# Two-layer decoder trunk on one core: the last dots moved ahead of the one-hot stage, value reads issued there, and a reordered RMSNorm

## Chip, cores and metric

One NeuronCore of a Trainium2 chip runs the whole program in one launch. The metric is device time in microseconds (us), the median of several runs. The program's engines are TensorE (PE; its weight loads are listed as PEld), VectorE (DVE), ScalarE (ACT), GpSimd (POOL) and SyncE (SP), which only issues DMAs here.

## What is computed

The reference runs two layers over 256 tokens of width 1024, then a final RMSNorm. A layer is: modulated RMSNorm, a token mixer (two kinds of attention, fed by one projection), a gated residual add, a second modulated RMSNorm, PEER expert retrieval and a second residual add. The part that the change touches most is PEER:

```
def rms_norm(x, g):
    y = x * lax.rsqrt(jnp.mean(x * x, axis=-1, keepdims=True) + RMS_EPS)
    return y * g
...
q = (ht @ wq).reshape(PEER_CHUNK, PEER_HEADS, 2, half)       # 8 heads
...                                                          # product keys: 16 of 16384 experts a head
act = jax.nn.gelu(jnp.einsum('td,thkd->thk', ht, u[e]))
return jnp.einsum('thk,thkd->td', gate * act, v[e])
```

Every token needs 8 x 16 = 128 rows of u and as many of v, out of tables of 16384 rows of 1024 floats each.

## The kernel before, in words

The kernel keeps the activations transposed in `xT` (eight tiles of 128 features by 256 tokens). One function writes each engine's instructions in the order of the source; nothing reorders them, and each engine and each DMA queue works through its own list in that order.

**PEER is done in two ways at once.** For the first 160 tokens (`ND`) TensorE multiplies with the whole tables: 128 tiles of u (512 KB each, 128 experts by 1024 features), a one-hot stage that turns the chosen experts and gates into a dense gate matrix, then 128 tiles of v. For the last 96 tokens (`NG`) GpSimd reads only the chosen rows by indirect DMA, 128 rows (512 KB) a read, 96 reads of u and 96 of v a layer. VectorE takes the dot product of each u read with the tokens (`dot`, L1236), ScalarE and VectorE turn the dots into weights (`weigh` L1240, `gated` L1243), and VectorE adds each v read, weighted, into one of two accumulators (`axpy`, L1250 and L1252). A v read can be issued when a dot or an axpy has given a buffer back; up to ten are in flight.

**In the order of the program**, `peer` has: 16 query units (L1351 to L1372); 128 u tiles (L1444), each followed by a Gelu on ScalarE (L1432) and by gather work that a build-time account of VectorE's time lets in (`fill`); the one-hot stage (L1456 to L1475), 40 rounds of four tokens, each with three one-hots on VectorE and one on GpSimd (L1409), a matmul (L1416, `spread_gates`) and a multiplication into the dense matrix on VectorE (L1475); 128 v tiles (L1506). The six queued tiles of v and ten more in spare memory are loaded in the one-hot stage, so sixteen lie ready when the v tiles begin.

Beside the v tiles the gather work that is left runs at a pace, `V_PACE`: a credit of 0.7 steps a tile up to tile 106 and 1.2 after it. Before each such step VectorE copies one column of the newest v tile asked for (`seen`, L1510), so that a step, and with it the read that it lets go, waits until that tile has landed. At tile 122 (`NI - GE`) all steps that are left are issued without that wait. After tile 124 (`NI - GP`) `gathered_part` (L1485) has TensorE fold the two accumulators onto the tokens (L1491): first the one whose buffer is named side, then the one named rows, each when its last axpy is done. Two tiles follow, then the sums of squares of the 96 tokens (L297), the last tile, the residual adds (L1482), the squares of the 160 tokens (L288) and their sums (L297).

**RMSNorm** is `rms_rstd` (L306): the sums of squares lie in a PSUM bank; ScalarE takes the reciprocal root of sum/1024 + epsilon (L312), VectorE forms sum/1024 + epsilon again (L313) and does one Newton step with it (L314 to L316). `busy` (L299) gives TensorE `W1` or `W2` idle matmuls beside that. `norm_mod` then forms the scale `gs` (L325) and the normalised tiles; after the mixer `norm_whole` (L352) makes them.

**Weights** pass through `feed` (L371): a loaded piece is cut into a high part on ScalarE (L395) and a low part, a subtraction on VectorE or GpSimd (L397). Ahead of the norm after the mixer, `want(pos[U_WQ])` (L1581) makes sure that three query units are cut, the third one's subtraction included.

## Time and profile before

| what | value |
|---|---|
| median of 3 runs | 1949.45 us (1948.42 to 1951.34) |
| the profiled execution's own time | 1956.64 us |
| its span | 1954.8 us |
| busy share of the span | PE 95%, PEld 91%, DVE 66%, POOL 29%, ACT 26% |
| data moved | 605.26 MB, mean 310 GB/s |
| mean granted TensorE clock | 0.971 of full |

All rows come from the profiled execution. Start times count from the start of its span. A timeline row is: start, duration, engine, line, operation, what it writes and reads, how many were merged, and in brackets the idle time just before it with what ended it. A TensorE operation in 32-bit floats has two records a matmul, so one v or u tile (eight matmuls) is 16 records.

### The profile page before, as it was taken

What the parts mean: (1) busy time and instruction counts of PE and PEld (TensorE: products, weight loads), DVE (VectorE), ACT (ScalarE), POOL (GpSimd) and SP (SyncE); (2) the same over time, 40 slices, a digit from 0 to 9 for tenths busy, and PEclk for the clock granted to TensorE, in tenths of its full rate; (3) what the DMA queues carried; (4) which work ended last, traced back from release to release, by engine and by line L of the source; (5) the groups of instructions that cost most, each with busy time, mean ns of one, the idle gap of its engine ahead of it and who ended that gap; (6) DMA issues with size and microseconds to landing.
All of it is one profiled execution on the core that took longest, in us unless ns stands there. A gap on an engine that the chain in (4) does not pass through costs nothing. (4 is left out here: it accounts for less than half of the span.)

```text
span 1954.8 us, 34450 instructions
## 1 busy us (share of the span) xinstructions
PE 1857.3 (95%) x13284; PEld 1779.2 (91%) x13284; DVE 1288.4 (66%) x3084; ACT 500.4 (26%) x1079; POOL 573.4 (29%) x524
## 2 busy tenths in 40 slices
PE   5899999999999999999879999999999999999996
PEld 4778898999999899999868799899999998999995
DVE  8788765789854854444765987578995458344456
ACT  3444545211211710000025554522111154000001
POOL 4000005245443533322400000243454344322341
PEclk7899999999999999999989999999999999999997
DMA  7767656899999379999926574589999974999993
GB/s 274 282 229 261 218 162 240 325 386 365 409 408 409 140 270 375 409 409 408 407 96 240 204 267 163 200 294 366 366 409 408 409 295 145 349 408 408 407 410 155
DMA packets 166484, 605.26 MB, mean 310 GB/s; under 512 B 18480, under 2 KB 19120, under 8 KB 166192
## 3 DMA queue, kind: packets, MB, share of 16 engines
q1 hardware_dynamic: 111024, 401.71, 54.8%
q0 software_dynamic: 55296, 201.35, 26.3%
q8 instruction: 105, 1.72, 0.4%
q14 instruction: 59, 0.48, 0.1%
HBM read 601.94 MB, written 1.05 MB: 308 GB/s over the span
## 5 line engine op out<-in xcount | busy, mean ns | idle before, releaser
L1506 PE MATMUL bank<-wide,piece 128*128 128x160 f32 x3904 | 535.8, 300 | 2.6 <-DVE wide L1475 2.6
L1506 PEld LDWEIGHTS bank<-wide,piece 128*128 128x128 f32 x3904 | 534.4, 191 | 3.0 <-DVE wide L1475 3.0
L1444 PE MATMUL bank<-whole,piece 128*128 128x160 f32 x2624 | 360.7, 299 | 0.7 <-issue 0.4
L1444 PEld LDWEIGHTS bank<-whole,piece 128*128 128x128 f32 x2624 | 357.5, 190 | 1.6 <-issue 1.6
L1215 POOL DMA_INDIRECT side<-in_u_dram,routes x140 | 164.1, 1172 | 263.5 <-DVE side L1236 161.6
L397 POOL TENSOR_TENSOR piece<-piece 128x1024 fp32r<-128x1024 f32 x28 | 68.2, 2442 | 530.3 <-ACT piece L395 526.9
L1510 DVE COPY seen<-piece 128x1 f32<-128x1 f32 x176 | 27.0, 153 | 294.1 <-DMA piece<-in_v_dram 285.8
L1215 POOL DMA_INDIRECT side<-in_v_dram,routes x134 | 135.3, 1010 | 281.2 <-DVE side L1252 170.1
L1444 PE MATMUL bank<-whole,wide 128*128 128x160 f32 x1472 | 205.5, 299 | 3.1 <-issue 3.1
L1444 PEld LDWEIGHTS bank<-whole,wide 128*128 128x128 f32 x1472 | 201.3, 190 | 3.6 <-issue 3.4
L1432 ACT ACTIVATE wide<-bank 128x160 f32<-128x160 f32 x256 | 77.7, 305 | 469.3 <-PE bank L1444 406.0
L420 PE MATMUL bank<-hHL,piece 128*128 128x256 f32 (+1 forms) x592 | 176.7, 299 | 17.5 <-ACT hHL L344 14.2
L421 PE MATMUL bank<-hHL,piece 128*128 128x256 f32 (+1 forms) x592 | 174.9, 295 | 5.5 <-POOL hHL L347 4.3
L422 PE MATMUL bank<-hHL,piece 128*128 128x256 f32 (+1 forms) x592 | 173.5, 293 | 4.5 <-DVE piece L397 3.4
L395 ACT ACTIVATE piece<-piece 128x1024 fp32r<-128x1024 f32 x140 | 146.3, 1062 | 98.6 <-issue 37.3
L397 DVE TENSOR_TENSOR piece<-piece 128x1024 fp32r<-128x1024 f32 (+1 forms) x112 | 138.3, 1240 | 49.5 <-ACT piece L395 43.3
L1236 DVE SCALAR_TENSOR_TENSOR side<-side 128x1024 f32<-128x1024 f32 x94 | 114.9, 1222 | 45.0 <-DMA side<-in_u_dram,routes 35.1
L420 PEld LDWEIGHTS bank<-hHL,piece 128*128 128x128 f32 (+1 forms) x592 | 117.5, 199 | 20.4 <-ACT hHL L344 15.1
L421 PEld LDWEIGHTS bank<-hHL,piece 128*128 128x128 f32 (+1 forms) x592 | 117.2, 198 | 9.4 <-POOL hHL L347 6.4
L422 PEld LDWEIGHTS bank<-hHL,piece 128*128 128x128 f32 (+1 forms) x592 | 117.5, 199 | 6.5 <-DVE piece L397 4.9
L1252 DVE SCALAR_TENSOR_TENSOR side<-side,routes 128x1024 f32<-128x1024 f32 x86 | 110.5, 1285 | 0.4 <-DMA side<-in_v_dram,routes 0.3
L261 DVE SCALAR_TENSOR_TENSOR wide<-wide 128x1024 f32<-128x1024 f32 x80 | 97.7, 1222 | 16.9 <-DMA wide<-in_w_ada_dram 16.9
(244 smaller groups left out, 2777.8 us busy)
## 6 DMA issues: line engine op xcount, KB each, us to landing
piece<-in_v_dram SPq DMA_DIRECT2D x244, 512.0 KB
piece<-in_uT_dram SPq DMA_DIRECT2D x164, 512.0 KB
piece<-in_W_dram SPq DMA_DIRECT2D x147, 512.0 KB
wide<-in_uT_dram SPq DMA_DIRECT2D x92, 512.0 KB
wide<-in_w_ada_dram SPq DMA_DIRECT2D x80, 512.0 KB
side<-in_w_ada_dram SPq DMA_DIRECT2D x16, 512.0 KB
wide<-in_v_dram SPq DMA_DIRECT2D x8, 512.0 KB
side<-in_u_dram,routes POOLq DMA_INDIRECT x140
```

Source lines behind the costliest of these rows:

```text
L261: nc.vector.scalar_tensor_tensor(buf(n), buf(n), 1.0, self.S["silu"], op0=OP.mult, op1=OP.mult, accum_out=self.mod[l][:, u:u + 1])
L395: nc.scalar.activation(Hs[i], raws[i], AF.Copy)
L397: self.subs.append(lambda: eng.tensor_sub(Ls[i], raws[i], Hs[i].bitcast(F32)))
L420: mm(out, l[0], r[0], start=start, stop=False, skip_group_check=True)
L421: mm(out, l[0], r[1], start=False, stop=False, skip_group_check=True)
L422: mm(out, l[1], r[0], start=False, stop=stop, skip_group_check=True)
L1215: nc.gpsimd.indirect_dma_start(out=r, out_offset=None, in_=self.a[table], in_offset=bass.IndirectOffsetOnAxis(ap=self.gidx[:, lot:lot + 1] ...
L1236: nc.vector.scalar_tensor_tensor(junk, box[n], 1.0, htok[a], op0=OP.mult, op1=OP.mult, accum_out=dots[:, lot:lot + 1])
L1252: nc.vector.scalar_tensor_tensor(acc[a], box[n], dots[:, lot:lot + 1], acc[a], op0=OP.mult, op1=OP.add)
L1432: nc.scalar.activation(dst(i - 1), ps.pop(i - 1)[:, :ND], AF.Gelu_apprx_tanh)
L1444: nc.tensor.matmul(p[:, :ND], w[:, k], self.whole[:, k, :ND], start=(k == 0), stop=(k == KC - 1))
L1506: nc.tensor.matmul(acc[k], r[:, k * 128:(k + 1) * 128], dst(i), start=i == 0 and k % 2 == 0, stop=i == NI - 1, skip_group_check=True)
```

## The change

It has three parts.

- **Gather.** At the last u tile the remaining dots, `weigh` and `gated` are issued at once, then `pump` issues reads of v into every free buffer. `V_PACE` becomes 1.25 a tile for 8 tiles and 0.74 after that, and the `seen` copy is left out for the first 8 tiles.
- **Norms.** Epsilon times 1024 is added to the sums by a matmul of one row (`epsd`), the first into the bank, so the root needs no bias and the Newton step reads the bank itself: L313 goes. The scale `gs` is formed ahead of the root (`norm_scale`). At the end of PEER the squares go to memory of the gather stage instead of a ring of three tiles. `W1` is 13 for 16 and `W2` 8 for 10. A copy at the start that nothing used (`identr`) goes.
- **Third query unit.** Its subtraction is put behind the norm's work, and its 24 matmuls are ordered so that the eight with the low part come last.

The diff, cut:

```
-W1 = 16
-W2 = 10
+W1 = 13
+W2 = 8
-V_PACE = (0.7, 106, 1.2)
+V_PACE = (1.25, 8, 0.74)
+        self.epsd = cp.tile([1, 128], F32, name="epsd")
+        nc.gpsimd.memset(self.epsd, EPS * D)
-    def sum_sq(self, k, lo=0, hi=SEQ):
-
-        sq = self.wk.tile([128, SEQ], F32, name="sq", tag="t2", bufs=3)[:, :hi - lo]
+    def sum_sq(self, k, lo=0, hi=SEQ, sq=None):
+
+        if sq is None:
+            sq = self.wk.tile([128, SEQ], F32, name="sq", tag="t2", bufs=3)[:, :hi - lo]
...
-            self.ss, start = self.bank(), True
-        else:
-            start = False
-        self.nc.tensor.matmul(self.ss[:, lo:hi], self.ones, sq, start=start, stop=k == KC - 1, skip_group_check=True)
+            self.ss = self.bank()
+            self.nc.tensor.matmul(self.ss[:, :SEQ], self.epsd, self.ones[0:1, 0:1].to_broadcast([1, SEQ]), start=True,
+                                  stop=False, skip_group_check=True)
+        self.nc.tensor.matmul(self.ss[:, lo:hi], self.ones, sq, start=False, stop=k == KC - 1, skip_group_check=True)
...
-        nc.scalar.activation(r, p, AF.Abs_reciprocal_sqrt, bias=self.epst, scale=1.0 / D)
-        nc.vector.tensor_scalar(v, p, 1.0 / D, EPS, op0=OP.mult, op1=OP.add)
+        nc.scalar.activation(r, p, AF.Abs_reciprocal_sqrt, scale=1.0 / D)
         nc.vector.tensor_mul(q, r, r)
-        nc.vector.scalar_tensor_tensor(q, q, -0.5, v, op0=OP.mult, op1=OP.mult)
+        nc.vector.scalar_tensor_tensor(q, q, -0.5 / D, p, op0=OP.mult, op1=OP.mult)
...
+    def norm_scale(self, l, which):
+
+        g = self.vec[:, V_L + l * V_LN + 48 + 8 * which:][:, :8]
+        self.gs = self.wk.tile([128, 8], F32, name="gs", tag="gs")
+        self.nc.vector.scalar_tensor_tensor(self.gs, self.mod[l][:, 24 * which + 8:24 * which + 16], 1.0, g, op0=OP.add,
+                                            op1=OP.mult)
...
+        if low_last:
+            for n, (a, b) in enumerate([(0, 0), (0, 1), (1, 0)]):
+                for k in range(KC):
+                    self.nc.tensor.matmul(out, w[a][:, k], self.h[k][:, b], start=n == 0 and k == 0,
+                                          stop=n == 2 and k == KC - 1, skip_group_check=True)
+            return
...
-                self.proj_T(p[:, :SEQ], w)
+                self.proj_T(p[:, :SEQ], w, low_last=j == 2)
...
+                if i == NI - 1:
+                    while self.weighed < 2 and gather():
+                        pass
+                    head(gathers)
+                    self.pump()
...
-            if credit[0] > 0 and head(gathers) is not None and i < NI - 9:
+            if credit[0] > 0 and head(gathers) is not None and V_PACE[1] <= i < NI - 9:
                 nc.vector.tensor_copy(seen, ahead[max(ahead)][:, 0:1])
...
-            sums.append(self.sum_sq(k, 0, ND))
+            sums.append(self.sum_sq(k, 0, ND, G[:, UNIT + k * ND:UNIT + (k + 1) * ND]))
...
+        self.put_off = True
         want(pos[U_WQ])
+        self.put_off = False
         self.norm_mod(l, 1)
+        self.flush()
```

What the diff does not tell is how many steps move. GpSimd's list around the one-hot stage (both layers alike; L1215 is the indirect read and L1409 the one-hot, in the changed file L1227 and L1423) is before:

```order
L1215 DMA side<-in_u_dram,routes 128x1024 x5
L1215 DMA rows<-in_v_dram,routes 128x1024
L1409 TENSOR_SCALAR piece<-cst,routes 128x128 x5
L1215 DMA rows<-in_v_dram,routes 128x1024
L1409 TENSOR_SCALAR piece<-cst,routes 128x128 x35
L1215 DMA side<-in_v_dram,routes 128x1024 x6
```

and now:

```order
L1227 DMA side<-in_u_dram,routes 128x1024 x5
L1227 DMA rows<-in_v_dram,routes 128x1024 x2
L1227 DMA side<-in_v_dram,routes 128x1024 x6
L1227 DMA rows<-in_v_dram,routes 128x1024
L1227 DMA side<-in_v_dram,routes 128x1024
L1423 TENSOR_SCALAR piece<-cst,routes 128x128 x40
```

Ten reads of v stand ahead of all 40 one-hots where one stood before, with a second after five one-hots. On VectorE at the same place (dots L1248, `gated` L1256, one-hots L1423, multiplication L1494 in the changed file), the changed list is:

```order
L1248 SCALAR_TENSOR_TENSOR side,routes<-rows 128x1024 x2
L1248 SCALAR_TENSOR_TENSOR side,routes<-side,rows 128x1024 x5
L1256 TENSOR_TENSOR routes<-routes 128x96
L1423 TENSOR_SCALAR piece<-cst,routes 128x128 x9
L1494 TENSOR_TENSOR wide<-wide,bank 128x128x4
```

The five dots and `gated` (L1256) stood behind the 40 rounds before, among the first v tiles. VectorE's list at the end of the v tiles of the first layer (copy `seen` L1510, axpy L1252, cut L397) is before:

```order
L1510 COPY seen<-piece 128x1
L1252 SCALAR_TENSOR_TENSOR rows<-side,routes,rows 128x1024 x5
L397 TENSOR_TENSOR piece<-wide,piece 128x1024 x2
L1252 SCALAR_TENSOR_TENSOR rows<-side,routes,rows 128x1024
L1252 SCALAR_TENSOR_TENSOR rows<-rows,routes 128x1024
L1252 SCALAR_TENSOR_TENSOR rows<-side,routes,rows 128x1024
L1252 SCALAR_TENSOR_TENSOR rows<-rows,routes 128x1024 x2
L1252 SCALAR_TENSOR_TENSOR rows<-side,routes,rows 128x1024 x4
```

and now (copy L1529, axpy L1266, cut L402):

```order
L1529 COPY seen<-piece 128x1
L1266 SCALAR_TENSOR_TENSOR rows<-rows,routes 128x1024
L1266 SCALAR_TENSOR_TENSOR rows<-side,routes,rows 128x1024 x3
L402 TENSOR_TENSOR piece<-wide,piece 128x1024 x2
L1266 SCALAR_TENSOR_TENSOR rows<-side,routes,rows 128x1024
```

Behind the last copy stood 14 axpys and now stand 5; nine more have a copy of their own ahead of it. The second layer is the same without the two cuts.

## Rows read from the trace of the kernel before

**Rows 1.** The page, its 40 equal slices of the span (48.9 us each): GB/s that the DMA engines moved.

```profile
GB/s 274 282 229 261 218 162 240 325 386 365 409 408 409 140 270 375 409 409 408 407 96 240 204 267 163 200 294 366 366 409 408 409 295 145 349 408 408 407 410 155
```

**Rows 2.** Waits of PE over the whole span: who waited for whom, us in total, times, longest.

```profile
PE bank L1491 <- DVE rows L1252: 27.5, 2, 16.3
PE bank L420 <- ACT hHL L344: 14.2, 2, 12.9
```

**Rows 3.** Timeline, end of the v tiles of the second layer (DVE and PE).

```profile
1910.14 0.15 DVE L1510 COPY seen<-piece 128x1 f32<-128x1 f32 x1 [1.17 <-DMA piece<-in_v_dram]
1910.24 7.89 DVE L1252 SCALAR_TENSOR_TENSOR rows<-side,routes,rows 128x1024 f32<-128x1024 f32 x6
...
1915.76 1.89 PE L1491 MATMUL bank<-cst,side 128*128 128x64 f32 x16
...
1923.45 5.25 DVE L1252 SCALAR_TENSOR_TENSOR rows<-side,routes,rows 128x1024 f32<-128x1024 f32 x4
...
1928.85 3.60 PE L1491 MATMUL bank<-cst,rows 128*128 128x32 f32 x16 [11.19 <-DVE rows L1252]
1932.26 6.42 PE L1506 MATMUL bank<-wide,piece 128*128 128x160 f32 x32
...
1938.51 1.92 PE L297 MATMUL bank<-side,ones 128*128 128x96 f32 x16
```

**Rows 4.** Timeline, end of the v tiles of the first layer (DVE and PE).

```profile
963.57 0.15 DVE L1510 COPY seen<-piece 128x1 f32<-128x1 f32 x1 [1.17 <-DMA piece<-in_v_dram]
963.68 6.57 DVE L1252 SCALAR_TENSOR_TENSOR rows<-side,routes,rows 128x1024 f32<-128x1024 f32 x5
...
968.33 1.89 PE L1491 MATMUL bank<-cst,side 128*128 128x64 f32 x16
...
970.16 2.36 DVE L397 TENSOR_TENSOR piece<-wide,piece 128x1024 fp32r<-128x1024 f32 x2
...
985.06 1.28 DVE L1252 SCALAR_TENSOR_TENSOR rows<-side,routes,rows 128x1024 f32<-128x1024 f32 x1 [0.28 <-DMA side<-in_v_dram,routes]
...
986.49 3.60 PE L1491 MATMUL bank<-cst,rows 128*128 128x32 f32 x16 [16.27 <-DVE rows L1252]
989.90 6.55 PE L1506 MATMUL bank<-wide,piece 128*128 128x160 f32 x32
...
996.29 1.92 PE L297 MATMUL bank<-side,ones 128*128 128x96 f32 x16
```

**Rows 5.** Stretches of time: bounds, length, busy time of PE, PEld, DVE, ACT and POOL with their instructions, then the granted clock of TensorE (1.00 is full), DMA share and GB/s.

```profile
986.00:990.00 4.00, 3.51 (x17) 3.54 (x17) 1.88 (x9) 0.00 (x0) 0.00 (x0) 0.50 0.00 0
990.00:996.00 6.00, 6.00 (x31) 6.00 (x31) 2.72 (x10) 4.23 (x5) 0.00 (x0) 0.67 0.00 0
996.00:1003.00 7.00, 7.00 (x54) 6.59 (x53) 3.51 (x9) 2.49 (x9) 2.47 (x3) 1.00 0.00 0
1928.00:1932.00 4.00, 3.15 (x15) 3.18 (x16) 2.24 (x9) 0.00 (x0) 0.00 (x0) 0.50 0.00 0
```

**Rows 6.** The chain that ended last, its longest piece: v tiles of the second layer without a break.

```profile
1643.99 252.39 PE bank L1506 x1856
```

**Rows 7.** Timeline, end of the u tiles and first one-hots of the second layer.

```profile
1564.49 0.94 POOL L1215 DMA_INDIRECT side<-in_u_dram,routes  x1 [1.61 <-DVE side L1236]
1565.56 1.23 DVE L1236 SCALAR_TENSOR_TENSOR side<-rows 128x1024 f32<-128x1024 f32 x1 [1.34 <-DMA rows<-in_u_dram,routes]
...
1567.06 0.94 POOL L1215 DMA_INDIRECT rows<-in_v_dram,routes  x1 [1.63 <-DMA piece<-in_uT_dram]
1568.11 1.23 DVE L1236 SCALAR_TENSOR_TENSOR side<-rows 128x1024 f32<-128x1024 f32 x1 [1.32 <-DMA rows<-in_u_dram,routes]
...
1586.10 0.30 ACT L1432 ACTIVATE wide<-bank 128x160 f32<-128x160 f32 x1 [2.20 <-PE bank L1444]
...
1589.99 1.05 PE L1416 MATMUL bank<-piece 128*128 128x128 f32 x8
...
1590.48 0.79 POOL L1409 TENSOR_SCALAR piece<-cst,routes 128x128 f32<-128x128 f32 x1 [14.75 <-PE bank L1416]
...
1591.15 0.69 DVE L1475 TENSOR_TENSOR wide<-wide,bank 128x512 f32<-128x512 f32 x1 [17.44 <-PE bank L1416]
...
1591.43 1.03 POOL L1215 DMA_INDIRECT rows<-in_v_dram,routes  x1 [0.16 <-issue]
...
1591.76 0.85 DVE L1409 TENSOR_SCALAR piece<-cst,routes 128x128 f32<-128x128 f32 x3
```

**Rows 8.** Norms. First the norm after the mixer of the second layer (DVE), and the idle matmuls beside it (PE).

```profile
1241.20 3.62 PE L303 MATMUL bank<-maskb,identb 128*128 128x512 bf16 x16
...
1241.91 0.43 DVE L313 TENSOR_SCALAR rms<-bank 128x256 f32<-128x256 f32 x1 [1.11 <-ACT rstd L312]
1242.25 0.42 DVE L314 TENSOR_TENSOR rms<-rstd 128x256 f32<-128x256 f32 x1
...
1243.50 1.22 DVE L397 TENSOR_TENSOR piece<-piece 128x1024 fp32r<-128x1024 f32 x1
...
1244.91 0.88 DVE L359 SCALAR_TENSOR_TENSOR h<-xT,gs,rstd 128x256 f32<-128x256 f32 x2
```

**Rows 9.** The chain that ended last: one sum-of-squares matmul of 256 columns in the mixer's output units. Then the timeline of the last norm: ScalarE's squares, held up by TensorE.

```profile
1232.56 0.43 PE bank L297 x2
...
1942.94 1.57 ACT L288 ACTIVATE sq<-xT 128x160 f32<-128x160 f32 x5 [0.56 <-PE bank L297]
```

More of the change, by code (lines that the diff above doesn't have):

```diff
@@ L178, in load_consts @@
         nc.gpsimd.tensor_copy(self.identb, self.ident)
-        self.identr = cp.tile([128, 128], F32R, name="identr")
-        nc.gpsimd.tensor_copy(self.identr, self.ident)
         self.iotab = cp.tile([1, 128], BF16, name="iotab")
@@ L310, in rms_rstd @@
         r = self.rstd = self.wk.tile([128, SEQ], F32, name="rstd", tag="rstd", bufs=1)
-        v, q = [self.wk.tile([128, SEQ], F32, name="rms", tag="t2", bufs=3) for i in range(2)]
-        nc.scalar.activation(r, p, AF.Abs_reciprocal_sqrt, bias=self.epst, scale=1.0 / D)
-        nc.vector.tensor_scalar(v, p, 1.0 / D, EPS, op0=OP.mult, op1=OP.add)
+        q = self.wk.tile([128, SEQ], F32, name="rms", tag="t2", bufs=3)
+        nc.scalar.activation(r, p, AF.Abs_reciprocal_sqrt, scale=1.0 / D)
         nc.vector.tensor_mul(q, r, r)
-        nc.vector.scalar_tensor_tensor(q, q, -0.5, v, op0=OP.mult, op1=OP.mult)
+        nc.vector.scalar_tensor_tensor(q, q, -0.5 / D, p, op0=OP.mult, op1=OP.mult)
         nc.vector.scalar_tensor_tensor(r, q, 1.5, r, op0=OP.add, op1=OP.mult)
         self.busy(fill)
+    def norm_scale(self, l, which):
[3 more added lines that the diff above has]
+                                            op1=OP.mult)
     def norm_mod(self, l, which, before=None, gs=None):
         nc = self.nc
-        g = self.vec[:, V_L + l * V_LN + 48 + 8 * which:][:, :8]
         m = self.mod[l][:, 24 * which:24 * which + 24]
         if not before:
-            gs = self.wk.tile([128, 8], F32, name="gs", tag="gs")
-            nc.vector.scalar_tensor_tensor(gs, m[:, 8:16], 1.0, g, op0=OP.add, op1=OP.mult)
+            gs = self.gs
         hHL = [self.st.tile([128, KC // 2, 2, SEQ], F32R, name="hHL", tag="h", bufs=2) for _ in range(2)]
@@ L422, in mm3, with proj_T @@
         mm(out, l[1], r[0], start=False, stop=stop, skip_group_check=True)
-    def proj_T(self, out, w, rhs=None, nk=KC):
+    def proj_T(self, out, w, rhs=None, nk=KC, low_last=False):
+        if low_last:
[4 more added lines that the diff above has]
+            return
         for k in range(nk):
@@ L978, in token_mixer @@
             s()
+        self.norm_scale(l, 1)
         self.rms_rstd(W1)
@@ L1240, in weigh @@
             nc.scalar.activation(dots, dots, AF.Gelu_apprx_tanh)
+            self.weighed = 1
         def gated():
             nc.vector.tensor_mul(dots, dots, self.ggate)
+            self.weighed = 2
         begun = set()
@@ L1297, in peer @@
         self.tv = self.tp = self.now = 0.0
-        self.rows = self.q_done = 0
+        self.rows = self.q_done = self.weighed = 0
         self.asked, self.routed, self.coded = [False, False], [False, False], [False, False]
@@ L1532, in peer @@
             self.S = self.layout_mixer(l + 1)
+        if l + 1 < DEPTH:
+            self.norm_scale(l + 1, 0)
         self.rms_rstd(W2)
```

## The prediction, made before the changed kernel ran

> **What bounds the kernel now.** The page comes first: PE is busy 95% of the span at a mean granted clock of 0.971, so time can only be won where PE stands still or runs below full clock. The list of PE's waits names such places: 27.5 us in two waits of the fold L1491 for axpys, and 14.2 us of the first projections for their normalised input [rows 2]. The chain of waits shows what lies ahead of the fold: in the second layer 1856 records of v tiles without a break in 252.39 us, which is 116 tiles of 16 records at 2.176 us [rows 6]. No transfer ends there last, but the slack is small: the slices of the v stage stand at 407 to 410 GB/s, the highest values of the page [rows 1]. At 409 GB/s 512 KB take 1.28 us; a tile and 0.7 reads take 2.18 us, as long as PE needs for the tile.
>
> The timelines of the two tails show why the fold waits. The last `seen` copy runs at 1910.14 (second layer) and 963.57 (first); behind it stand 14 axpys, and the last end at about 1928.7 and 986.3. PE has the side accumulator folded at 1915.76 + 1.89 = 1917.65 and 968.33 + 1.89 = 970.22, and then stands for 11.19 and 16.27 us [rows 3, 4]. When it goes on, the granted clock is 0.50, the lower of its two levels (1.2 of 2.4 GHz), and full again from about 994 in the first layer [rows 5].
>
> **Term 1, the wait for the axpys.** The change leaves five axpys behind the last copy. An axpy takes 7.89 / 6 = 1.32 us [rows 3]. If the last awaited tile lands when it did, the second layer's five end at 1910.24 + 6.6 = 1916.8, ahead of PE at 1917.65: no wait. In the first layer four axpys end at 968.9, the two cuts (2.36 us [rows 4]) at about 971.3 and the fifth axpy at 972.6, so PE would wait 2.4 us. Does the landing stay? Before, tiles past 106 let 1.2 reads go a tile, now 0.74: over 12 tiles 0.46 x 12 x 1.28 = 7.1 us less on the queues. Against it, a tile with 0.74 reads takes 1.74 x 1.28 = 2.23 us, 0.05 more than PE needs; over about 100 tiles that is 5 us. The two leave the landing some 2 us earlier. I take half of the first layer's 2.4: 27.5 - 1.2 = **26.3 us** won; the bounds are 27.5, and 14.7 if the whole 5.6 us of rival A falls due.
>
> **Term 2, the lower clock after the wait.** From the fold's second part to the last sums takes 1928.85 to 1938.51 = 9.66 us in the second layer and 986.49 to 996.29 = 9.80 in the first. At full clock it is at most 1.89 for the fold (the side part, which is longer, took that) and two tiles and the start of the sums behind them, 2 x 2.176 = 4.35: 6.24 us [rows 3, 4, 6]. With no wait there is no fall: 3.42 + 3.56 = **7.0 us** won. If a wait of 1 or 2 us is left the clock may hold all the same: beside ScalarE's squares PE stood for about that long in the trace, and the tail of the first layer was at 1.00 [rows 5, 9]. The lower bound is 0.
>
> **Term 3, the norms.** After the mixer, L313 goes, 1242.25 - 1241.91 = 0.34 us; the third unit's subtraction and `gs` stood between the Newton step and `h`, from 1243.50 to 1244.91 = 1.41 us, of which about 0.12 stays as start-up of the next instruction [rows 8]. That is 1.63. The epsilon matmul costs what one sum of 256 columns does, at most 0.43 [rows 9]. Net 1.2 us, twice: 2.4. The subtraction that goes behind is 1.22 us of DVE, and it is covered: the third unit needs it for its last eight matmuls only, when two units and sixteen matmuls lie ahead. At the end of PEER L313 goes again (0.34), and squares no longer wait for a tile of their ring (0.56 [rows 9]); less 0.43 that is about 0.5 a layer, with `gs` earlier in the first 0.6: 1.1 in all. The first norm, inside the 14.2 us of [rows 2], gains 0.3 at most. The idle matmuls are fewer (13 for 16, 3.62 / 16 = 0.23 us each [rows 8]): 3 us still stand in the gap, and the norm's chain behind them is shorter than before. Sum **3.8 us**, bounds 0 (if the 0.43 falls on the chain and `h` waits for ScalarE) and 5.
>
> **Term 4, the place where the work goes.** The dots issued at the last u tile must end before VectorE's first one-hots, and ten reads now stand in POOL's list ahead of its one-hots. Before, POOL issued the last u read at 1564.49, and DVE's last two dots there ran at 1565.56 and 1568.11, 2.55 us apart, the pace of reads that alternate with tiles [rows 7]. Five more at 2.55 start by 1580.9 and end by 1582.2. DVE had 17.44 us of idle time in this place [rows 7], so five dots of 1.23 cost it nothing. The last reads that dots let go are four issues of 0.94 to 1.03 [rows 7], hence done by 1582.5 + 4.1 = 1586.6, and POOL's first one-hot (0.79) can stand by 1587.5; PE took it up with its matmul at 1589.99. `weigh` stands on ScalarE behind the Gelu of the last but one tile (1586.10, 0.30), so `gated` can end at about 1587.0, the three one-hots of the first round (0.85) at 1587.9, and all nine that stand ahead of the first multiplication at 1589.6, where that multiplication, L1475, came at 1591.15 [rows 7]. The margin is 1.5 to 2.5 us. I charge 0.5 a layer, **1.0 us** lost; the bounds are 0, and 3 a layer, if the fifth dot comes two pairs of transfers (5.1) later than counted.
> The five dots, `weigh` and `gated` that stood among the first v tiles leave them; VectorE has room there, so that wins nothing. Transfers: eight reads more in the one-hot stage are 10.2 us of the queues, and the slice there was at 145 GB/s [rows 1].
>
> What a read's issue costs beside VectorE is seen once: 1.03 us at 1591.43, just ahead of VectorE's one-hots of 1591.76, against 0.94 with VectorE idle [rows 7]. By these rows it is 0.1 us an issue, inside the margin. The Trainium skill ("SBUF — State Buffer", section "SBUF: two separate sides") says that GpSimd cannot write a transfer's descriptors while VectorE copies 32-bit floats within SBUF, and names about 3100 ns for a transfer that takes 620 alone; by it four issues would take 12.4 us, the one-hot would come 5.8 us past 1589.99 in each layer, and the sum would be about 11 us smaller. The rows here show nothing of that size, and no issue in them lies wholly beside a dot.
>
> **Sum.** -26.3 - 7.0 - 3.8 + 1.0 = -36.1 us. The profiled execution's own time is 1956.64, so 1920.5 for it; it stands 7.2 above the median of the runs, 1949.45, which gives **1913.3 us** (-1.85%).
>
> **Rivals.**
> *A, the transfers fall behind.* The 0.05 us a tile add up over 110 tiles to 5.6 us, and the relief past tile 106 does not come because the backlog still has to drain. Then the last awaited tile lands 5.6 later, the second layer waits 1916.8 + 5.6 - 1917.65 = 4.8 us and the first 2.4 + 5.6 = 8.0: 12.8 in place of the 1.2, so 1913.3 + 11.6 = 1925; with the clock lost again 7 more, 1932. For it: the queues are at their limit already [rows 1]. Against it: with ten reads ahead of the one-hots fewer are left for the tiles, and the pace runs out of steps at the end. 12%.
> *B, reads hold up POOL.* If each of the four issues has to wait out the dot beside it, it takes 0.94 + 1.23 = 2.17 us [rows 7], POOL's one-hots come 4.6 us later, at about 1592.1, and PE stands 2.1 us in each layer: 4.2, less the 1.0 charged: 1916.5. If two dots stand in the way of each, 9.5 later and 7.0 a layer: 1926. For it: reads and dots now alternate there as nowhere before. Against it: the issue of 1.03 [rows 7]. The Trainium skill's rule above is the one that speaks for it. 8%.
> *C, slower: reads starve the tiles.* Reads without the `seen` wait fill their queue and, if the later pace keeps it full, a tile lands every 2 x 1.28 = 2.56 us where PE needs one every 2.176. Over the 96 - 10 = 86 reads left this is 33 us a layer. A stock of 16 tiles, 16 x 2.176 = 34.8 us, covers that; the case decides when fewer than about 7 tiles lie ready at the first v tile, for then over 18 us a layer fall through, as much as the sum wins. With no stock it is 66 - 36.1 = 30 us slower, 1979. For it: reads now go ahead of the stock's loads. Against it: the stock is loaded where the queues stood at 145 GB/s [rows 1], and PE did not break once in 116 tiles [rows 6]. 4%.
> *D, it does not do what it says:* the fifth axpy in the first layer comes late for another reason, since its read was the last to land there before (985.06, 0.28 after its data [rows 4]); then the first layer keeps half of its 16.27 us and the 3.56: 1913.3 + 7 + 3.56 = 1924. 6%.
>
> **How the numbers follow.** The forecast has 70%, A 12, B 8, D 6, C 4. The forecast's own range is 1907 (no wait left, norms at their upper bound, nothing lost in the gap, and the 3 us by which the three runs spread) to 1920 (6 lost in the gap, half of the norms' gain). The range goes to 1927, which takes in A without the clock's fall, B and D, and leaves out C and the rest of A; below it goes 2 us further, since how far one profiled execution stands above the median is known from one alone: 1905 to 1927. A change of 0.2% (3.9 us) is about what can be told from none. All cases but C are faster by more: faster 0.94, same 0.02, slower 0.04.
>
> **What would show it.** Right: the waits of PE at the fold under 3 us together; no stretch at 0.50 behind it; five axpys behind the last copy; no L313, and `h` right behind the Newton step; PE's first one-hot matmul after the last u tile no later against the last Gelus than before; v tiles unbroken at 2.176 us. Wrong: a fold that waits over 4 us (A, D), POOL's first one-hot as what PE or VectorE waits for after the u tiles (B), or v tiles that wait for their transfers (C).

## The result and the profile after

| | before | changed |
|---|---|---|
| median, the four runs that go with the prediction | 1950.39 us (1948.42 to 1952.63) | 1924.93 us (1918.03 to 1925.88) |
| ratio to before | | 0.9855, interval 0.9835 to 0.9874 |
| ratio in three later comparisons (5, 6 and 5 runs) | | 0.9834, 0.9837, 0.9843 |
| the profiled execution's span | 1954.8 us | 1916.2 us |
| mean granted clock of it | 0.971 | 0.986 |

The changed kernel is 1.5 to 1.7% faster, 25 to 34 us, where 36 were forecast and 1913.3 us. The first median, 1924.93, lies inside the stated range (1905 to 1927) but outside the forecast's own (1907 to 1920); the medians of the three later comparisons, 1916.40 to 1919.85, lie inside both. The direction and the places are those of the prediction; one term is too small, and one conversion was wrong. The page lists 34430 instructions; PE is busy 96% of its shorter span.

Among the waits of PE the fold for the axpys, 27.5 us before [rows 2], no longer stands. One that was not there before has come, for POOL's one-hot, which the prediction had named as the sign of rival B (us in total, times, longest):

```profile
PE bank L1430 <- POOL piece L1423: 3.0, 2, 2.7
```

**The tails**, from the fold to the last sums. The timeline of the changed kernel, first layer and then second, to be laid beside [rows 4] and [rows 3] (axpy L1266, copy L1529, cuts L402, fold L1510, v tiles L1525, epsilon's matmul L296, sums L298):

```profile
956.62 0.15 DVE L1529 COPY seen<-piece 128x1 f32<-128x1 f32 x1
...
958.07 3.93 DVE L1266 SCALAR_TENSOR_TENSOR rows<-side,routes,rows 128x1024 f32<-128x1024 f32 x3
961.91 2.35 DVE L402 TENSOR_TENSOR piece<-wide,piece 128x1024 fp32r<-128x1024 f32 x2
964.18 1.28 DVE L1266 SCALAR_TENSOR_TENSOR rows<-side,routes,rows 128x1024 f32<-128x1024 f32 x1
...
966.92 1.89 PE L1510 MATMUL bank<-cst,side 128*128 128x64 f32 x16
968.65 1.92 PE L1510 MATMUL bank<-cst,rows 128*128 128x32 f32 x16
...
974.93 0.70 PE L296 MATMUL bank<-ones,epsd 1*128 1x256 f32 x2
975.56 2.02 PE L298 MATMUL bank<-side,ones 128*128 128x96 f32 x16
...
1882.84 0.15 DVE L1529 COPY seen<-piece 128x1 f32<-128x1 f32 x1
...
1884.28 5.25 DVE L1266 SCALAR_TENSOR_TENSOR rows<-side,routes,rows 128x1024 f32<-128x1024 f32 x4
...
1891.93 1.89 PE L1510 MATMUL bank<-cst,side 128*128 128x64 f32 x16
1893.67 1.92 PE L1510 MATMUL bank<-cst,rows 128*128 128x32 f32 x16
```

The two parts of the fold now stand behind one another without a gap. The last axpy ends at 965.46 and at 1889.53, that is 3.2 and 4.1 us before PE asks for the accumulator. The last copy runs 10.3 and 9.1 us ahead of the fold, where it was 4.8 and 5.6 [rows 4, 3]: the awaited tile has landed 5.5 and 3.5 us earlier against PE. From the second part of the fold to the last sums it takes 975.56 - 968.65 = 6.91 us, of which 0.63 is the epsilon matmul; before it was 9.80 and 9.66 [rows 4, 3]. The stretches of the same execution (bounds, length, busy time of PE, PEld, DVE, ACT and POOL, granted clock, DMA share, GB/s) are at full clock where [rows 5] have 0.50:

```profile
966.00:970.00 4.00, 4.00 (x37) 4.00 (x36) 1.15 (x6) 0.00 (x0) 0.00 (x0) 1.00 0.10 38
970.00:977.00 7.00, 7.00 (x53) 6.50 (x52) 3.71 (x13) 4.23 (x5) 0.00 (x0) 1.00 0.00 0
1892.00:1902.00 10.00, 10.00 (x80) 9.49 (x78) 2.98 (x16) 2.33 (x3) 0.00 (x0) 1.00 0.01 2
```

**The norm after the mixer**, second layer, VectorE, beside [rows 8]:

```profile
1219.31 0.43 DVE L314 TENSOR_TENSOR rms<-rstd 128x256 f32<-128x256 f32 x1 [0.94 <-ACT rstd L313]
...
1220.77 0.88 DVE L364 SCALAR_TENSOR_TENSOR h<-xT,gs,rstd 128x256 f32<-128x256 f32 x2
```

From the Newton step's first operation to `h` it takes 1.46 us, before 1244.91 - 1242.25 = 2.66. With the 0.34 of the old L313 that is 1.54 less, where 1.63 were forecast.

**The one-hots**, first layer: POOL's last four early reads (the seventh to the tenth) and its first one-hots; the last dot, `gated` (L1256) and the one-hots on VectorE; PE's last u tile and first one-hot matmul. Then, from the second layer, the last dot, the tenth read and the last u tile:

```profile
631.35 0.95 POOL L1227 DMA_INDIRECT side<-in_v_dram,routes  x1 [1.61 <-DVE side L1248]
632.60 1.01 POOL L1227 DMA_INDIRECT side<-in_v_dram,routes  x1 [0.30 <-ACT wide L1446]
633.91 0.94 POOL L1227 DMA_INDIRECT rows<-in_v_dram,routes  x1 [0.30 <-issue]
636.88 0.94 POOL L1227 DMA_INDIRECT side<-in_v_dram,routes  x1 [2.02 <-PE bank L1458]
637.86 4.81 POOL L1423 TENSOR_SCALAR piece<-cst,routes 128x128 f32<-128x128 f32 x6
...
629.84 1.23 DVE L1248 SCALAR_TENSOR_TENSOR side<-side,rows 128x1024 f32<-128x1024 f32 x1 [1.32 <-DMA side<-in_u_dram,routes]
...
632.53 0.26 DVE L1256 TENSOR_TENSOR routes<-routes 128x96 f32<-128x96 f32 x1 [1.45 <-ACT wide L1446]
632.90 2.58 DVE L1423 TENSOR_SCALAR piece<-cst,routes 128x128 f32<-128x128 f32 x9
...
633.74 2.34 PE L1458 MATMUL bank<-whole,piece 128*128 128x160 f32 x16
638.74 1.23 PE L1430 MATMUL bank<-piece 128*128 128x128 f32 x8 [2.66 <-POOL piece L1423]
...
1557.73 1.23 DVE L1248 SCALAR_TENSOR_TENSOR side<-side,rows 128x1024 f32<-128x1024 f32 x1 [1.33 <-DMA side<-in_u_dram,routes]
...
1563.52 0.94 POOL L1227 DMA_INDIRECT side<-in_v_dram,routes  x1 [0.85 <-DMA piece<-in_v_dram]
...
1562.72 2.34 PE L1458 MATMUL bank<-whole,piece 128*128 128x160 f32 x16
```

VectorE is done with its nine one-hots at 635.5. POOL issues three reads 1.25 and 1.31 us apart, and then stands 2.02 us ahead of the tenth; its one-hots begin 1.8 us after PE's last u tile (633.74 + 2.34 = 636.08), and PE waits 2.66 us. The last dot ends at 629.84 + 1.23 = 631.07, that is 5.0 us ahead of the end of the last u tile, and in the second layer at 1558.96, 6.1 us ahead of 1565.06; the forecast had 8.0 (1582.2 against 1587.82 + 2.34 = 1590.16). The clock falls in the same place:

```profile
636.00:639.00 3.00, 0.34 (x3) 0.27 (x3) 0.00 (x0) 0.79 (x2) 2.08 (x3) 1.00 1.01 397
639.00:644.00 5.00, 5.00 (x28) 4.20 (x28) 2.57 (x7) 3.13 (x6) 4.03 (x6) 0.66 1.02 408
```

### The profile page after: what moved, and what is told of

Read it like the earlier page. It is cut to its first block, busy times and chain, and to the rows that moved or that the text cites. A ratio compares the mean times of both kernels' runs of the same rounds, so it can differ in the third digit from the quotient of the medians.

```text
span 1916.2 us, 34430 instructions
## 1 busy us (share of the span) xinstructions
PE 1847.3 (96%) x13284; PEld 1766.9 (92%) x13284; DVE 1285.6 (67%) x3067; ACT 500.4 (26%) x1079; POOL 564.9 (29%) x524
## 5 line engine op out<-in xcount | busy, mean ns | idle before, releaser
L1525 PE MATMUL bank<-wide,piece 128*128 128x160 f32 x3904 | 532.0, 299 | 2.6 <-DVE wide L1494 2.6
L1525 PEld LDWEIGHTS bank<-wide,piece 128*128 128x128 f32 x3904 | 530.6, 190 | 3.0 <-DVE wide L1494 3.0
L1227 POOL DMA_INDIRECT side<-in_u_dram,routes x140 | 163.4, 1167 | 266.2 <-DVE side L1248 164.1
L402 POOL TENSOR_TENSOR piece<-piece 128x1024 fp32r<-128x1024 f32 x28 | 68.4, 2448 | 521.7 <-ACT piece L400 500.6
L1529 DVE COPY seen<-piece 128x1 f32<-128x1 f32 x164 | 25.1, 153 | 277.0 <-DMA piece<-in_v_dram 264.8
L1227 POOL DMA_INDIRECT side<-in_v_dram,routes x134 | 129.6, 967 | 234.6 <-DVE side L1266 114.7
L425 PE MATMUL bank<-hHL,piece 128*128 128x256 f32 (+1 forms) x576 | 171.1, 297 | 13.6 <-ACT hHL L349 11.7
L426 PE MATMUL bank<-hHL,piece 128*128 128x256 f32 (+1 forms) x576 | 169.6, 294 | 7.5 <-POOL hHL L352 6.3
L427 PE MATMUL bank<-hHL,piece 128*128 128x256 f32 (+1 forms) x576 | 167.8, 291 | 4.7 <-DVE piece L402 3.6
L402 DVE TENSOR_TENSOR piece<-piece 128x1024 fp32r<-128x1024 f32 (+1 forms) x112 | 138.2, 1239 | 44.8 <-ACT piece L400 40.3
L1248 DVE SCALAR_TENSOR_TENSOR side<-side 128x1024 f32<-128x1024 f32 x94 | 114.8, 1222 | 46.7 <-DMA side<-in_u_dram,routes 35.1
L425 PEld LDWEIGHTS bank<-hHL,piece 128*128 128x128 f32 (+1 forms) x576 | 113.0, 196 | 16.8 <-ACT hHL L349 12.6
L426 PEld LDWEIGHTS bank<-hHL,piece 128*128 128x128 f32 (+1 forms) x576 | 112.6, 196 | 12.1 <-POOL hHL L352 8.3
L427 PEld LDWEIGHTS bank<-hHL,piece 128*128 128x128 f32 (+1 forms) x576 | 113.0, 196 | 6.9 <-DVE piece L402 5.3
L1266 DVE SCALAR_TENSOR_TENSOR side<-side,routes 128x1024 f32<-128x1024 f32 x86 | 110.6, 1286 | 0.5
L261 DVE SCALAR_TENSOR_TENSOR wide<-wide 128x1024 f32<-128x1024 f32 x80 | 97.6, 1221 | 17.9 <-DMA wide<-in_w_ada_dram 17.7
```

Of the source, the lines that this page charges most:

```text
L261: nc.vector.scalar_tensor_tensor(buf(n), buf(n), 1.0, self.S["silu"], op0=OP.mult, op1=OP.mult, accum_out=self.mod[l][:, u:u + 1])
L402: self.subs.append(lambda: eng.tensor_sub(Ls[i], raws[i], Hs[i].bitcast(F32)))
L425: mm(out, l[0], r[0], start=start, stop=False, skip_group_check=True)
L426: mm(out, l[0], r[1], start=False, stop=False, skip_group_check=True)
L427: mm(out, l[1], r[0], start=False, stop=stop, skip_group_check=True)
L1227: nc.gpsimd.indirect_dma_start(out=r, out_offset=None, in_=self.a[table], in_offset=bass.IndirectOffsetOnAxis(ap=self.gidx[:, lot:lot + 1] ...
```

## The experiments

The kernels were timed in three later comparisons, each on one chip and each with the kernel before; the three medians of before stand in their order. In the first were norms only, the whole gather part, the changed kernel again and the 24 memsets; in the second pace only, early dots and reads only, the changed kernel a third time and nine reads; the others in the third. The first row of the changed kernel is that of the result. Span is that of the profiled execution. The fold is the time from the start of its first part to the end of its second, first and second layer; without a wait it is 3.65 us. The last column is from PE's last u matmul to its first one-hot matmul, first and second layer (-0.16: no wait).

| kernel | median us | ratio (interval) | span us | fold us | one-hots wait us |
|---|---|---|---|---|---|
| before | 1948.7, 1951.6, 1949.4 | 1 | 1954.8 | 21.76, 16.69 | -0.16, -0.16 |
| norms only | 1946.45 | 0.9986 (0.9975 to 0.9997) | 1944.4 | 21.55, 16.45 | -0.16, -0.16 |
| pace only | 1942.19 | 0.9956 (0.9942 to 0.9970) | 1942.0 | 16.19, 13.23 | -0.16, -0.16 |
| early dots and reads only | 1929.86 | 0.9893 (0.9872 to 0.9914) | 1932.1 | 8.16, 8.09 | 1.39, 1.71 |
| whole gather part only | 1920.85 | 0.9856 (0.9842 to 0.9870) | 1919.3 | 3.65, 3.65 | 2.03, 1.43 |
| changed, first | 1924.93 | 0.9855 (0.9835 to 0.9874) | 1916.2 | 3.65, 3.66 | 2.66, 0.39 |
| changed, again | 1916.40 | 0.9834 (0.9820 to 0.9847) | 1912.2 | 3.65, 3.65 | 2.01, 1.15 |
| changed, third | 1917.44 | 0.9837 (0.9816 to 0.9858) | 1912.2 | 3.65, 3.65 | 1.69, 1.17 |
| changed, fourth | 1919.85 | 0.9843 (0.9828 to 0.9858) | 1920.4 | 3.65, 3.65 | 2.65, 1.98 |
| 24 memsets on POOL | 1919.94 | 0.9846 (0.9832 to 0.9861) | 1915.7 | 3.65, 3.65 | 1.37, 1.62 |
| ten reads, buffers swapped | 1915.19 | 0.9834 (0.9811 to 0.9858) | 1913.4 | 3.65, 3.65 | 3.09, 1.29 |
| nine reads | 1913.41 | 0.9808 (0.9788 to 0.9829) | 1911.9 | 3.65, 3.65 | -0.16, -0.16 |
| nine reads, again | 1914.16 | 0.9808 (0.9786 to 0.9829) | 1914.7 | 3.65, 3.66 | -0.16, -0.16 |
| nine reads, more idle matmuls | 1910.41 | 0.9794 (0.9777 to 0.9811) | 1910.6 | 3.65, 3.65 | -0.16, -0.16 |

**The gather part alone** is the kernel before with this:

```
-V_PACE = (0.7, 106, 1.2)
+V_PACE = (1.25, 8, 0.74)
...
+                if i == NI - 1:
+                    while self.weighed < 2 and gather():
+                        pass
+                    head(gathers)
+                    self.pump()
...
-            if credit[0] > 0 and head(gathers) is not None and i < NI - 9:
+            if credit[0] > 0 and head(gathers) is not None and V_PACE[1] <= i < NI - 9:
```

> The kernel before with the gather part alone (dots, weigh, gated and reads at the last u tile, the new pace). Theory, the blind sum: 27.5 us of waiting at the fold and 7.0 of the lower clock go, 1 is lost at the one-hots, so -33 against before (1917). Rival 1, the gather part gives something back at the one-hots: the first POOL one-hot waited for 2.66 us in the first layer of the changed kernel's profile, and if both layers lose this and the clock behind it, -24 (1926), and the norms' part is worth the whole 4. Rival 2, the norms' part costs time: gather alone -33 or more, and norms alone slower than before. The fold's waits are under 1 us in all of them.

It is 27.9 us faster than before. The list of PE's waits has no fold, and the new wait is there. The gain lies between the theory's 33 and rival 1's 24:

```profile
PE bank L1418 <- POOL piece L1411: 3.5, 2, 2.0
```

**The norms alone** are the changed kernel with that part undone.

> The changed kernel with the gather part undone (old pace, dots behind the one-hots). Theory: -3.8 us against before (1946.6), of it 1.2 at each norm after the mixer and 1.1 at the two ends of PEER. Rival 2: the epsilon matmul (0.63 us start to start in the changed kernel's trace, not 0.43) and fewer idle matmuls take that back or turn it round: 0 to +5 us. The fold's two waits stay at 27 us together.

The fold waits as before, the ratio's interval means 0.6 to 4.9 us faster, 2.3 by the medians; on top of the gather part (1920.85 to 1916.40) it is 4.4. Rival 2, no gain or a loss, falls, though its matmul is real: 0.63 us where I took at most 0.43.

```profile
PE bank L1505 <- DVE rows L1266: 27.0, 2, 16.1
```

**Early dots and reads without the new pace, and the new pace without them.** The first has the block at the last u tile, the second the other two lines of the diff above.

> The kernel before with the early dots and reads, at its old pace (0.7 a tile to tile 106, then 1.2) and with its seen copies: seven axpys stand behind the last copy in place of 14. Theory (what stands behind the last copy, times 1.32 us, is the wait): 7 x 1.32 = 9.2 us less of axpys in each layer, the second layer's fold waits 2 us at most, the first's 5 to 7, the clock falls in the first layer at most; 18 to 26 us faster than before, by one-hots' 3.5 us less. Rival: the pace is what makes the last tiles land in time; without it 1.2 reads a tile at the end keep the landing where it was or later, and the gain is under half of gather_only's 28.

> The kernel before with the new pace (1.25 a tile for 8 tiles without the seen copy, then 0.74) alone; dots stay behind the one-hots. 12 axpys stand behind the last copy in place of 14. Theory: 2.6 us less of axpys and a landing up to 3 us earlier a layer: the fold's waits fall from 27 to about 16 to 22 us, the clock still falls behind both, 5 to 11 us faster than before. Rival: the pace is the main thing: over 15 us faster.

By the ratios they give 21 and 9 us alone and 28 together, so the two nearly add up, the early dots are the larger part, and neither alone removes the wait. The waits of the fold are 6.0 us in the first kernel and 18.5 in the second (before: 27.5); the order's count of axpys behind the last copy is 7 and 12 (before: 14; changed: 5). Waits of the first kernel and its tail in the first layer, then the clock there:

```profile
PE bank L1498 <- DVE rows L1254: 6.0, 2, 3.4
...
971.10 2.60 DVE L1254 SCALAR_TENSOR_TENSOR rows<-side,routes,rows 128x1024 f32<-128x1024 f32 x2
...
973.84 2.88 PE L1498 MATMUL bank<-cst,rows 128*128 128x32 f32 x16 [3.39 <-DVE rows L1254]
```

```profile
974.00:980.00 6.00, 6.00 (x29) 6.00 (x29) 2.59 (x15) 1.83 (x3) 0.00 (x0) 0.55 0.08 31
```

A wait of 3.39 us was enough here for a stretch near 0.50 behind it. From the second part of the fold to the last sums this layer takes 9.53 us, against 6.19 in the whole gather part, so the lower clock cost 3.3 us, as much as the wait. One step of the expectation was wrong: the second layer waits 2.6 us, and the clock falls there too (9.31 us). The waits of the second kernel:

```profile
PE bank L1491 <- DVE rows L1252: 18.5, 2, 10.7
```

**Why POOL is late.** My first theory was its code: 8 KB of it were transferred at 636.55, while POOL stood. 24 memsets ahead of PEER move where in POOL's list a piece of code ends:

```
+        if l == 0:
+            for _ in range(24):
+                nc.gpsimd.memset(self.pad, 0.0)
```

> The changed kernel with 24 tiny memsets on POOL ahead of PEER in the first layer, which move where in POOL's list its next piece of code ends. Theory: in the changed kernel POOL stood from 634.8 to 636.6 between two reads because its code was loaded then (8 KB on queue 14 at 636.55), so with the shift the 2.66 us wait of PE for POOL's one-hot in the first layer and the 3.4 us stretch at 0.50 behind it go: 3 to 4.5 us faster than the changed kernel. Rival: the tenth read waits for a place in its queue or for a landing; then the wait stays within 0.5 us of what it was, and the time within 0.1%.

The theory falls: the median is not lower (1919.94 against 1916.40 in the same comparison, with intervals that overlap), and POOL stands idle ahead of the tenth read for the same time to a tenth of a microsecond, though the 8 KB came at 640.39 here, 1.06 us after the tenth read had started. PE's wait is shorter (1.37 us for 2.66) since the last dot ended 6.3 us ahead of the u tiles' end instead of 5.0:

```profile
636.29 0.94 POOL L1228 DMA_INDIRECT rows<-in_v_dram,routes  x1 [0.30 <-ACT routes L1253]
639.33 0.94 POOL L1228 DMA_INDIRECT side<-in_v_dram,routes  x1 [2.10 <-issue]
```

Next, the buffer: in the changed kernel the tenth read goes into the scratch buffer of the dots. This gives that buffer to the eighth:

```
-                free += [*htok, junk]
+                free += [junk, *htok]
```

> The changed kernel, with the last three buffers of the early reads given out in another order: the dots' scratch buffer goes to the eighth read, not to the tenth. Theory 1, the number of reads in flight: the tenth still stands 1.8 us (first layer) and 0.5 (second) on POOL, and the time is that of the changed kernel. Theory 2, that one buffer: the eighth read stands instead and the tenth goes on at once; the eighth comes so early that PE's wait for the one-hots falls by up to those 1.8 and 0.5 us.

The tenth stands as before, the eighth does not:

```profile
630.53 0.94 POOL L1227 DMA_INDIRECT side<-in_v_dram,routes  x1 [0.30 <-DMA rows<-in_v_dram,routes]
631.78 1.00 POOL L1227 DMA_INDIRECT side<-in_v_dram,routes  x1 [0.30 <-ACT piece L1412]
634.86 0.94 POOL L1227 DMA_INDIRECT rows<-in_v_dram,routes  x1 [2.09 <-ACT piece L1412]
```

So it is not the buffer, and the releasers that the timeline infers there (PE, ScalarE, none) change from run to run while the stand does not. Last, one read fewer ahead of the one-hots:

```
-        def pump():
+        def pump(keep=0):
...
-            while free and open_to(n):
+            while len(free) > keep and open_to(n):
...
-                    self.pump()
+                    self.pump(1)
```

> The changed kernel, but the last of the ten early reads is left for the middle of the one-hot stage. In four traces POOL stands 1.8 us (first layer) and 0.5 (second) ahead of the tenth read, and its one-hots come behind it. Theory: the tenth read waits because over five reads are in flight, so with nine POOL is at its one-hots 3.0 and 1.8 us earlier, PE's wait for them (1.2 to 2.7 us in the first layer, 0.4 to 1.6 in the second) goes, and the time falls by 3 to 6 us against the changed kernel in the same call. Rival 1: any last read, the ninth too, stands before the switch to one-hots; then 1 to 2 us. Rival 2: what the one-hots wait for is not POOL but weigh, gated and VectorE's one-hots; then no difference within 0.1%.

> The version with nine early reads once more. Theory: 3 to 5 us below the changed kernel of this call, with no wait of PE for the one-hots in either layer; the one comparison so far gave 1913.4 against 1917.4 with intervals that overlap.

```profile
633.53 0.95 POOL L1227 DMA_INDIRECT side<-in_v_dram,routes  x1 [0.30 <-DMA rows<-in_v_dram,routes]
634.78 0.94 POOL L1227 DMA_INDIRECT rows<-in_v_dram,routes  x1 [0.30 <-DMA piece<-in_v_dram]
635.76 4.03 POOL L1423 TENSOR_SCALAR piece<-cst,routes 128x128 f32<-128x128 f32 x5
639.96 1.03 POOL L1227 DMA_INDIRECT side<-in_v_dram,routes  x1 [0.17 <-issue]
...
635.95 2.34 PE L1458 MATMUL bank<-whole,piece 128*128 128x160 f32 x16
638.12 1.05 PE L1430 MATMUL bank<-piece 128*128 128x128 f32 x8
```

No read waits, POOL's one-hots begin 2.5 us ahead of the end of PE's last u tile (635.95 + 2.34), where they began 1.8 behind it, and PE goes from the u tiles into them without a wait, in both layers. In two comparisons this is 4.0 and 5.7 us below the changed kernel by the medians, though the intervals of the ratios touch (0.9788 to 0.9829 and 0.9786 to 0.9829 against 0.9816 to 0.9858 and 0.9828 to 0.9858); in the second its slowest run, 1916.80, is below the changed kernel's fastest, 1917.45. The traces agree: from the end of the u tiles to the fold it is 325.7 to 326.0 us in every layer of the three traces with nine reads, 327.1 to 330.8 in the first layer and 326.9 to 329.5 in the second of the changed kernel's four, and 325.6 before.

That PE's wait goes with the tenth read is shown; why the tenth stands is not. The number of reads in flight, the theory of the expectation, does not explain it alone. In the eight traces with ten early reads the tenth starts 2.96 to 3.08 us after the ninth in the first layer and 1.76 to 1.81 in the second, and the transfer records have 4.6 to 5.0 earlier reads still to land at that moment in the first layer and 5.0 to 5.4 in the second, while the ninth, which never stood, started with 4.7 to 5.1. In the first layer the tenth thus waits on with no more reads in flight than the ninth started with.

**Idle matmuls.** The nine-read version with `W1 = 16` and `W2 = 10`:

> The version with nine early reads, with the idle matmuls of before (16 and 10 for 13 and 8). Theory: PE's gap in the norms is not filled by either number, so the end of the norm's chain sets the time: same within 0.1%, and the stretches at 0.50 stay as they are. Rival: the fewer matmuls let the clock fall for 3.4 to 6.8 us behind a norm (1027 in three traces); with 16 and 10 those go and it is 2 to 4 us faster. Other rival: 16 of 0.23 us reach past the shorter chain and cost 0.7 us each, 2 to 3 us in all.

1910.41 against 1914.16 in the same comparison, with runs that overlap (1908.2 to 1913.7, 1906.7 to 1916.8). Nothing speaks for a cost of the idle matmuls; that they help is not shown, and the stretch at 0.50 at 1027 us that the first rival wanted to remove stands in this trace too. It is the lowest median of all.

**The changed kernel again.**

> The changed kernel once more. Its profiled execution took 1918.0 us at a mean granted clock of 0.986, three other executions 1924.5 to 1925.9 at 0.981 to 0.982. Theory: the 7 us are one more long stretch at 0.50 (about 20 us of it, since the clock's mean is lower by 0.005), in a place of its own that a trace of an execution at 0.981 would show as one stretch. Rival: they are several stretches of 3.4 us at different short waits of PE, as the trace of before has seven of them ahead of 310 us and at 1052 to 1216. If this profile again stands at 0.986, neither is decided.

> The changed kernel once more, to stand beside nine_reads in one call, and on whatever chip this call gets. If it is near 1916 again, 1924.9 was the draw of that first comparison; near 1925, chips or calls differ by that much. Its waits at the one-hots are expected at 1.2 to 2.7 us in the first layer and 0.4 to 1.6 in the second.

> The changed kernel once more, beside the three others of this call. Expected near the 1916.4 and 1917.4 of the last two calls; the waits at the one-hots 1.2 to 2.7 us in the first layer and 0.4 to 1.6 in the second.

The profiled executions of the second and the third time took 1914.0 us; the fourth's took 1922.1 at 0.979, and shows where 8 us lie:

```profile
641.00:644.00 3.00, 3.00 (x12) 2.30 (x12) 1.15 (x4) 0.75 (x2) 2.70 (x4) 0.50 1.03 411
...
968.00:972.00 4.00, 4.00 (x36) 4.00 (x35) 1.77 (x9) 0.00 (x0) 0.00 (x0) 0.96 0.06 24
972.00:975.00 3.00, 3.00 (x13) 3.00 (x13) 1.22 (x8) 1.75 (x2) 0.00 (x0) 0.50 0.00 0
...
1569.00:1572.50 3.50, 3.50 (x17) 2.80 (x16) 1.55 (x4) 1.83 (x4) 3.10 (x5) 0.51 1.02 404
```

There are several short stretches at 0.50. Two stand behind the wait for the one-hots; the one in the first tail stands behind no wait at all, since PE was busy all of the 4 us ahead of it. By PE's stages against the execution of 1912.2 us span: the wait at the one-hots 0.64 and 0.83 us longer, the one-hot stages behind them 1.49 and 1.54 longer, the first tail 1.68, the part ahead of the u tiles 1.76. The rival is right for this execution. Why the first comparison's three other runs came out at 1924.5 to 1925.9, some 2 us above any of the 16 since, stays open: no trace shows them.

## Why the prediction was nearly right, and where it was not

The mechanism of the gain was right: the wait for the axpys and the lower clock behind it went, for the reason forecast. The price at the one-hots was too small, and the step from one execution to the median did not hold.

**Term 1** (26.3 us, bound 27.5): right. All 27.5 us of the fold's waits are gone. The one step that was wrong is on the safe side: the landing came not 2 us but 5.5 and 3.5 us earlier against PE, so the first layer waits for nothing.

**Term 2** (7.0): right. The tails take 6.28 us without the epsilon matmul, against 9.80 and 9.66: 6.9 us. The early-dots kernel shows that it hangs on the wait: with 3.39 us of waiting left, the clock was at 0.55 behind it. "With no wait there is no fall" is too strong, though: of the 20 tails in the ten traces whose fold does not wait, three had a stretch of about 3 us at 0.50 all the same and took 8.6 us for 6.9 (first layer of the fourth time and of the swapped buffers, second of nine reads again). Why is open.

**Term 3** (3.8, bounds 0 to 5): right within what could be measured, 2.3 and 4.4 by two pairs of medians. The two norm timelines give 1.54 for the 1.63 of the norm after the mixer. The epsilon matmul was under-sized (0.63).

**Term 4** (1.0, bounds 0 to 6): the mis-sized term. It had POOL's first one-hot done 2.5 us before PE needs it; in the first layer it came 2.7 us too late. Two of its steps failed together.

- *When the u tiles end against the reads.* "Five more at 2.55 start by 1580.9 and end by 1582.2" was right about the dots: from the start of the last read of u to the end of the last dot it is 17.6 us in both layers of the changed kernel's first trace, where the forecast had 17.7. But PE's last u tile ended 25.7 us after the start of that read in the layer that the forecast read, and 22.6 and 23.7 us after it in the changed kernel. In all thirteen traces other than that of before this time is 22.4 to 24.2 us, without the early dots too, so the forecast had built on the longest of the values, from one execution. The last dot thus ends 4.4 to 6.3 us ahead of the u tiles' end in the eight traces with ten early reads, for the 8.0 forecast.
- *How long four issues take.* "The last reads that dots let go are four issues of 0.94 to 1.03" took it that reads follow one another at 1 us. They start 1.25 to 1.31 us apart, and the fourth, the tenth early read, starts 1.8 us later than that in the first layer and 0.5 in the second. The four took 636.88 + 0.94 - 631.35 = 6.5 us there, not 4.1, and 5.2 in the second.

In these eight traces PE's wait and the time by which the last dot is ahead add up to 7.7 us in the first layer and 6.4 to 6.5 in the second. With the 8.0 forecast PE would not have waited even for the slow issues; with issues as fast as forecast it would have waited 0.9 us at most. PE waits 1.4 to 3.1 us in the first layer and 0.4 to 2.0 in the second; with the clock behind it this cost 4 to 6 us, what the nine reads give back.

That is rival B's place and size (4.2 to 14 us), but not its mechanism: the four issues took 0.94 to 1.01, and no dot ran beside them, since the last one had ended at 631.07. The sentence of the Trainium skill, "SBUF — State Buffer", section "SBUF: two separate sides", on GpSimd held up while VectorE copies 32-bit floats is not tested by them, for no such copy ran there either. Yet B was not without ground: in the trace of before 53 of the 192 reads of u took over 1.2 us, one beside dots at 463.56 even 2.17, which is B's price, and so did 13 reads of v, this one beside two axpys:

```profile
1889.79 2.61 DVE L1252 SCALAR_TENSOR_TENSOR side<-side,routes 128x1024 f32<-128x1024 f32 x2
...
1891.34 1.86 POOL L1215 DMA_INDIRECT side<-in_v_dram,routes  x1 [1.61 <-DVE side L1252]
```

Others beside an axpy took 1.01 (1893.51), so what decides is not shown. The prediction's rows had none of the long ones.

**Rivals A and C** fell: the transfers did not fall behind, and the v tiles take 271.77 us from the first to the fold in both layers of before's trace and of all twelve kernels timed later, 272.5 and 272.3 in the changed kernel's first. D fell: the fifth axpy ended 3.2 us early.

**The conversion to the median** was the weak step of the sum. I took it that the profiled execution stands 7.2 us above the median in both kernels. The profiled executions of the changed kernel stood 6.9, 2.4 and 3.5 us below the medians of their comparisons and 2.3 above. That of before had eight short stretches at 0.50 outside the tails, the changed kernel's first had two besides the one at the one-hots. One of them in the trace of before:

```profile
1052.00:1055.00 3.00, 2.90 (x7) 2.33 (x8) 1.34 (x4) 1.06 (x1) 0.00 (x0) 0.50 0.93 351
```

How many an execution has differs from one to the next. So it is in part luck that the changed kernel's first profiled execution, 1918.03, came within 2.5 us of the 1920.5 forecast for it: the way from the u tiles to the folds cost it 6.5 us (330.84 and 326.87 us, for 325.6 before), where term 4 had charged 1.0. Six short stretches fewer, at 1.5 to 1.7 us each an estimate of 9 to 10 us, made up for it. By spans of the profiled executions the gain is 34 to 43 us; by medians 25 to 34. The sum of 36 had term 4 too small by some 3 to 5 us, which leaves 31 to 33, as in the three later comparisons (32.3, 34.1, 29.5); against the first comparison's 25.5 some 6 us remain that no trace explains.

## What to carry to other kernels

Work behind a semaphore that only paces something is worth counting: what stands in an engine's list behind the last such wait, times its duration, bounds the wait of the engine that needs it, and each piece moved ahead of it won time and, once little was left, the clock behind it. When work is moved into another engine's idle stretch, two things make the margin: the spacing of the instructions in the trace, not their durations, and how far the two engines stand apart there, which differed by some 3 us between executions here. A sum made against one profiled execution says little about a median within 0.4%: compare several executions first.

## What the runs showed of the hardware

- GpSimd reads that follow one another start 1.23 to 1.32 us apart though each takes 0.94 to 1.01. The fourth in such a row, the tenth early read, started 2.96 to 3.08 us after the one before it in the first layer and 1.76 to 1.81 in the second, in all eight traces with ten early reads, whatever its buffer and whatever POOL did before.
- A read that starts beside a dot or an axpy of 128x1024 can take 1.8 to 2.2 us on GpSimd (1.86 at 1891.34 and 2.17 at 463.56 in the trace of before) where it takes 0.94 alone; others beside one took 1.01 (1893.51).
- A wait of PE was followed by a stretch of about 3 us or more at 0.50 in some executions (1.98, 2.03, 2.65 and 3.39 us here) and by none in others (2.01 us ahead of the first layer's one-hots in the changed kernel's second trace, 3.09 with the swapped buffers). In three tails such a stretch came with no wait ahead of it. Each of the short ones cost 1.5 to 1.7 us.
